# Wider first projections, other PSUM places and two small moves in a sparse-attention block on one core

## The chip, the cores and the metric

The kernel runs on one core of a Trainium2 chip. A core has five engines that work side by side: TensorE (PE in the profile, with its weight loads shown apart as PEld), VectorE (DVE), ScalarE (ACT), GpSimd (POOL) and SyncE (SP), which here issues most of the DMAs. Each engine takes its instructions in order and waits on semaphores for the others. Matmul results land in PSUM, which has eight banks of 512 f32 columns; all other tiles lie in SBUF. The metric is the device time of one execution in microseconds (us).

## What is computed

One layer of a streaming-encoder block on 4096 tokens with 1024 features, in float32:

```python
h = rms_norm(x, norm_g)                 # (4096, 1024)
proj = h @ w_in                         # columns: q 512, k 128, v 128, qi 256, ki 32, wi 8,
                                        #          z_a 512, u_b 512, z_b 512, gates 2 x 1024
q, k = rope(rms_norm(q)), rope(rms_norm(k));  qi, ki = rope(qi), rope(ki)
iscore = sum_h relu(qi_h @ ki.T) * wi_h       # indexer score of every allowed key
idx = top_k(iscore, 256)                      # 256 keys for each query
a = softmax(q @ k[idx].T / 8) @ v[idx] * silu(z_a)
b = pool(u_b) * silu(z_b)                     # trailing means over 2, 4, 8, 16 tokens, a linear map
y = sigmoid(g_a) * (a @ w_branch_a) + sigmoid(g_b) * (b @ w_branch_b)
out = x + y @ w_out
```

A key is allowed if its chunk of 64 tokens does not come after the query's.

## The kernel before

The 4096 tokens are 32 tiles of 128. To come near f32 accuracy, an operand of a product is split into a high part (rounded to a shorter format, by ACT) and a low part (the rest, by DVE or POOL), and a product is three matmuls: high x high, low x high, high x low.

Four phases follow one another. **Phase 1** (`phase1`) normalises the token tiles, transposes them on PE, and projects them on the q, k/v and indexer columns (512, 256 and 296 columns of `w_in`). **The search** (`phase_index`) computes the indexer scores, searches a threshold for each query by iterating, and on the side computes the dense projections (`dense`: gates, pooling). A count of the queries where the threshold is not exact is kept in `cnt`; where it is above zero, `phase_exact` computes those blocks again by 32 rounds of "best eight, then strike them out" (`exact_block`, lines 1266 to 1268). **The attention** (`phase_attention`) and **the output** (`phase_out`) follow.

Within a phase the order on each engine is written by a planner (`Plan`): a step has an engine, an estimated cost, a key (its due time) and the steps that it waits for. `Plan.run` plays the steps through by these estimates and, whenever an engine is free, writes the ready step with the smallest key. So the costs and keys decide the order of the instructions; on the chip the engines then run that order at their real pace. Buffers are rings; a ring's tile gets its address when it is first made, so the order in which tiles are made decides which bank of PSUM they lie in. At the end of phase 1 the planner's remaining work of each engine (`self.left`, `self.late`) is handed to the plan of the search. A tile that lies where a tile of the phase before lay waits for that tile's last reader.

The steps that the change touches:

- `begin` (lines 284 to 313) sets a few constants, keeps PE warm with 18 matmuls on a zeroed tile, and spreads the norm gain `gn` over 128 partitions: ACT's queue loads it as one row into a tile of the ring `x`, PE multiplies it with a row of ones into a PSUM tile `ma`, DVE copies it out.
- Tiles 0 and 1 are projected while the weights arrive. `first` (line 639) is the order in which token tiles and pieces of the weights are loaded on SP's queue; a piece is at most 128 columns wide. `weights` (line 494) loads a piece, has ACT make its high part and DVE its low part; for the first and third q piece POOL makes the low part (`ON_POOL`).
- `piece` (line 515) multiplies a tile with one such piece: 24 matmuls, for each of the three products eight blocks of 128 features. The loop in lines 653 to 661 calls it for tiles 0 and 1 in turn and puts the transposes of tiles 2 and 3 in between. Tiles 2 to 31 go through `project`, whose matmuls are as wide as the column group (512, 256 or 296).
- PSUM in phase 1: two `ma` (two banks each, q and k/v), two `mb` (one bank, indexer), two `pt` (one bank, transposes). `evac` reads `ma` and `mb` and frees them; its last read of `ma` is line 557.
- PSUM in the search: two `ps` of two banks (scores), three `pd` of one (dense), one `pt` (transposes), made in the order that line 814 lists.
- `tables` (line 315) makes the rotation's sines and cosines on DVE and ACT; `evac` needs them before it can free its row buffer (`row`, two of them).
- At the attention's begin DVE sets the tile `ones` (line 1298), and ACT applies an exponential to one column of it (line 1309), so that its table is loaded.

Of the kernel before, what the change touches and what calls it, by code (L numbers as in the profile page):

```python
# [110 lines left out]
ON_POOL = {("q", 0), ("q", 2)}  # L111
# [144 lines left out]
class K:  # L256
# [6 lines left out]
    def consts(self):  # L263
# [6 lines left out]
        self.ii = c1.tile([P, P], I32, name="ii")  # L270
        self.ident = ci.tile([P, P], F32, name="ident")
# [12 lines left out]
    def begin(self, pl, sp, xp, gn):  # L284
# [3 lines left out]
        new = pl.new  # L288
        one = sp.tile([P, 1], F32, name="one")
        row = xp.tile([1, P], F32, name="onerow")  # L290
        s = pl.add("dve", 0.2, -100, lambda: (v.memset(one, 1.0), v.memset(row, 1.0)))
# [13 lines left out]
        x, ma = new("x"), new("ma")  # L305
        g = pl.add("dma", 0.1, -101, lambda: act.dma_start(x.t[0:1], a["norm_g"]), use=[x])

        def spread():
            for f in range(2):
                fs = slice(f * 512, f * 512 + 512)  # L310
                pe.matmul(ma.t[:, fs], row, x.t[0:1, fs], start=True, stop=True)
        g = pl.add("pe", 1.8, -60, spread, [g, s], use=[x, ma])
        return pl.add("dve", 1.2, -60, lambda: v.tensor_copy(gn, ma.t), [g], use=[ma])
# [91 lines left out]
    def phase1(self):  # L405
# [7 lines left out]
        with ExitStack() as es:  # L413
# [80 lines left out]
            def weights(key, j, at):  # L494
# [9 lines left out]
                on = "pool" if (key, j) in ON_POOL else "dve"  # L504
                eng = {"dve": v, "pool": po}[on]
                l = pl.add(on, (2.4 if on == "pool" else 1.15) * n + 0.1, at, lambda: eng.tensor_tensor(
# [8 lines left out]
            def piece(t, key, j, at, prev):  # L515
                m, c = out_of(t, key)
                o, e, hi, lo = pieces[key][j]
# [3 lines left out]
                for i, (x, w, after) in enumerate(((hh, wh, high + [hi]), (hl, wh, low), (hh, wl, [lo]))):  # L521
# [3 lines left out]
                    prev = pl.add("pe", 8 * 0.5e-3 * max(e - o, 64), at, mm, after + [prev], use=[m, hh, hl])  # L525
# [111 lines left out]
            for f in range(2):  # L637
                transp(0, f, -35 + f)
            first = (("q", 0), ("q", 1), ("x", 1), ("q", 2), ("q", 3), ("x", 2), ("kv", 0), ("kv", 1), ("x", 3), ("i", 0), ("i", 1),
                     ("i", 2))  # L640
# [12 lines left out]
            for n, (key, j) in enumerate(x for x in first if x[0] != "x"):  # L653
                for t in range(2):
                    last[t] = piece(t, key, j, n + t * 2.5, last[t])
                    if (key, j) == ("kv", 1):
                        ends[t] = last[t]
                if key == "kv":
                    transp(2, j, n + 2.0)
                elif key == "i" and j < 2:  # L660
                    transp(3, j, n + 4.0)
# [1559 lines left out]
```

## Time and profile before

| | us |
|---|---|
| median of 3 runs | 4133.96 (4132.86 to 4137.76) |
| profiled execution | 4135.42 |
| its span, first to last instruction | 4133.7 |
| PE busy | 4012.3 (97%) |
| DVE busy | 3251.7 (79%) |
| ACT busy | 2259.5 (55%) |
| POOL busy | 2022.9 (49%) |

An instruction's row gives its start and its length in us, the engine, the line of the kernel, the operation, its tiles as output <- inputs, their shapes, and how many were merged into the row; in brackets stands how long the engine idled before it and what it was released by. A `q` behind an engine's name marks its sequencer or DMA queue. Matmuls overlap, so the time of one in a stream is read from the distance between starts. The granted clock is the share of full speed at which PE was allowed to run.

### The profile page before, as it was taken

How to read it: one execution, taken by the hardware profiler on the slowest of the kernel's cores; microseconds unless marked ns; L12 is line 12 of the kernel's file. 1: busy time of each engine (PE TensorE's matmuls, PEld its weight loads, DVE VectorE, ACT ScalarE, POOL GpSimd, SP SyncE). 2: the span in 40 equal slices, each digit the busy share in tenths (PEclk: the TensorE clock that was granted, in tenths of full speed). 3: DMA queues.
4: the chain of work that ended last, by engine and by line, in shares of the span. 5: the costliest groups of instructions: out<-in, count | busy, mean ns of one | idle time of the engine just before them, and what ended most of it. 6: DMA issues, size and time to landing. Idle time of an engine off the chain costs nothing.

```text
span 4133.7 us, 64472 instructions
## 1 busy us (share of the span) xinstructions
PE 4012.3 (97%) x23202; PEld 3074.1 (74%) x23203; DVE 3251.7 (79%) x6399; ACT 2259.5 (55%) x3163; POOL 2022.9 (49%) x1618
## 2 busy tenths in 40 slices
PE   9999999999999999999989999999999999999999
PEld 9999888787777777788756666666666666887787
DVE  5555688888888888778779999999999996556654
ACT  4444578786777877877645555555554543111221
POOL 3555312212213223010018889999999994334653
PEclk9999999999999999999979999999999999999999
DMA  6876644544545345666554433333222215887543
GB/s 183 301 244 237 201 168 173 171 167 168 177 164 194 135 172 180 199 234 237 199 142 87 76 76 61 64 62 54 56 54 43 40 25 167 284 254 239 190 158 122
DMA packets 515846, 636.87 MB, mean 154 GB/s; under 512 B 230593, under 2 KB 365377, under 8 KB 511554
## 3 DMA queue, kind: packets, MB, share of 16 engines
q1 hardware_dynamic: 490432, 609.51, 47.1%
q10 hardware_dynamic: 25090, 23.21, 2.5%
q8 instruction: 183, 3.00, 0.3%
q14 instruction: 141, 1.16, 0.1%
HBM read 408.96 MB, written 191.76 MB: 145 GB/s over the span
## 4 chain that ended last, share of the span: by engine, by line
PE 37%; DVE 6%; issue 4%; DMA 1%; POOL 1%; SPq 1%; ACT 0%; ACTq 0%; DVEq 0%; POOLq 0%
PE pv L1686 9%; PE st L1634 8%; PE p L2139 7%; PE p L1990 7%; PE ps L1566 4%; DVE jk L1575 4%; DVE tt L1647 1%; PE pt L1734 1%; PE pt L395 1%; DMA qm<-maxD 1%; PE st L395 0%; PE st L1854 0%; POOL g L2020 0%; DVE w L1897 0%; DMA g<-w_out 0%
## 5 line engine op out<-in xcount | busy, mean ns | idle before, releaser
L1665 POOL TENSOR_TENSOR acc<-acc,tt 128x1024 f32<-128x1024 f32 x388 | 927.7, 2391 | 64.0 <-ACT tt L1646 36.9
L1646 ACT ACTIVATE tt<-tt 128x1024 f32<-128x1024 f32 (+1 forms) x544 | 561.1, 1034 | 549.7 <-DVE tt L1647 518.9
L1197 PE MATMUL pd<-h,wgh 128*128 128x512 f32 x1792 | 708.8, 396 | 9.9 <-DMA h<-hD 9.9
L1196 PE MATMUL pd<-h,wgh 128*128 128x512 f32 x1792 | 714.1, 399 | 3.9 <-issue 3.8
L908 DVE SCALAR_TENSOR_TENSOR ring<-rl,wi,ring 128x1024 f32<-128x1024 f32 (+7 forms) x624 | 702.1, 1170 | 15.7 <-ACT rl L906 12.4
L1198 PE MATMUL pd<-h,wgl 128*128 128x512 f32 x1792 | 707.0, 395 | 0.0
L906 ACT ACTIVATE rl<-ps 128x1024 f32<-128x1024 f32 (+7 forms) x624 | 535.5, 887 | 190.0 <-PE ps L903 69.4
L1647 DVE TENSOR_TENSOR tt<-st,bT 128x1024 f32<-128x1024 f32 (+1 forms) x504 | 600.8, 1193 | 13.1 <-PE st L1634 13.1
L993 ACT ACTIVATE sg<-ring,tk 128x2048 fp8e4<-128x2048 f32 (+9 forms) x322 | 485.1, 1508 | 63.0 <-DVE tk L981 34.4
L1686 PE MATMUL pv<-tt,vv 128*64 128x256 f32 x4224 | 516.2, 386 | 1.4 <-ACT ov L1707 1.4
L1575 DVE CUSTOM_DVE_ANT_1 jk<-ps,bias,mf 128x1024 bf16<-128x1024 f32 (+3 forms) x408 | 469.6, 1151 | 17.1 <-PE ps L1566 15.3
L1686 PEld LDWEIGHTS pv<-tt,vv 128*64 128x64 f32 x4224 | 286.5, 137 | 168.7 <-issue 35.4
L1197 PEld LDWEIGHTS pd<-h,wgh 128*128 128x128 f32 x1792 | 339.8, 190 | 84.1 <-DMA h<-hD 16.6
L1196 PEld LDWEIGHTS pd<-h,wgh 128*128 128x128 f32 x1792 | 340.0, 190 | 78.6 <-issue 4.2
L1198 PEld LDWEIGHTS pd<-h,wgl 128*128 128x128 f32 x1792 | 339.4, 189 | 75.9
L903 PE MATMUL ps<-kis,qT 128*128 128x512 f32 (+3 forms) x1136 | 345.3, 390 | 37.9 <-ACT rl L906 37.7
L1990 PE MATMUL p<-g,w 128*128 128x512 f32 x1488 | 345.5, 394 | 1.7 <-DVE g L1913 1.7
L1990 PEld LDWEIGHTS p<-g,w 128*128 128x128 f32 x1488 | 279.4, 188 | 67.6 <-DVE g L1913 2.1
L2139 PE MATMUL p<-w,g 128*128 128x512 f32 x1344 | 314.3, 396 | 4.0 <-ACT g L2143 3.1
L2139 PEld LDWEIGHTS p<-w,g 128*128 128x128 f32 x1344 | 253.5, 189 | 64.6 <-ACT g L2143 3.5
L1566 PE MATMUL ps<-kh,qh 64*128 64x512 f32 (+3 forms) x1320 | 265.5, 419 | 29.3 <-DVE mf L1575 26.5
L1110 POOL COPY halo<-u 128x16 f32<-128x16 f32 x32 | 11.2, 350 | 575.5 <-ACT u L1104 575.5
(364 smaller groups left out, 7012.3 us busy)
## 6 DMA issues: line engine op xcount, KB each, us to landing
h<-hD SPq DMA_DIRECT2D x384, 512.0 KB
g<-gD SPq DMA_DIRECT2D x80, 512.0 KB
hlD<-rhl SPq DMA_DIRECT2D x31, 1216.0 KB
gD<-sgm SPq DMA_DIRECT2D x128, 256.0 KB
q<-hlD SPq DMA_DIRECT2D x61, 512.0 KB
x<-x SPq DMA_DIRECT2D x32, 512.0 KB
hD<-hh SPq DMA_DIRECT2D x32, 512.0 KB
hD<-hl SPq DMA_DIRECT2D x32, 512.0 KB
```

The source lines that it names most:

```text
L906: r = pl.add("act", 0.05 + n * 0.834e-3, k_, lambda ps=ps, rl=rl, n=n: act.activation(rl.t[:, :n], ps.t[:, :n], AF.Relu), [m], use=[ps, rl])
L908: prev[o] = pl.add("dve", 0.1 + n * 1.04e-3, k_, lambda rl=rl, o=o, n=n, h=h: v.scalar_tensor_tensor(acc[:, o:o + n], rl.t[:, :n], self.wi ...
L1196: pe.matmul(out, wh.t[:, k], r1, start=(k == 0), stop=False)
L1197: pe.matmul(out, wh.t[:, k], r2, start=False, stop=False)
L1198: pe.matmul(out, wl.t[:, k], r1, start=False, stop=(k == KT - 1))
L1575: v.tensor_tensor_reduce(out=jk.t[:, :2 * (hi - lo) * P].rearrange("p (t n) -> p t n", t=2), in0=flat().rearrange("p (t n) -> p t n", t=2) ...
L1646: act.activation(tt.t[:, 0:n], tt.t[:, 0:n], AF.Exp)
L1647: ad = last_ve[0] = pl.add("dve", 0.07 + 0.54 * n, key, lambda: v.tensor_tensor(tt.t[:, 0:n], s.t[:, 0:n], bc(bt.t[:, 2 * p:2 * p + n, Non ...
L1665: gp.tensor_tensor(acc.t, first, tt.t, op=OP.add)
L1686: pe.matmul(pv.t[64 * f:64 * f + 64], vv[:, k, 64 * g:64 * g + 64], T[u, p].t[:, k % 2, 2 * f:2 * f + 2], start=(k == 0), stop=(k == b))
L1990: pe.matmul(p.t, blk[i].t[:, k, ms], two(x[k // 2][j].t, F32R)[:, k % 2], start=(k == i == j == 0), stop=(k == 3 and i == 1))
L2139: pe.matmul(p.t, quarter(Q.t, x, F32R)[:, k], blk[y].t[:, k], start=(fresh and k == x == y == 0), stop=(k == 3 and x == 1), skip_group_che ...
```

## The change

- `begin` no longer spreads the gain on PE. SP's queue loads it straight to all partitions, with a DMA that reads the same row 128 times, second in the queue.
- `ON_POOL` is gone: DVE makes all low parts of the weights.
- `piece` takes several weight pieces at a time: tiles 0 and 1 multiply q in two halves of 256 columns, k/v in one of 256, the indexer's columns in one of 296. The weights still arrive in pieces of 128 columns, the token tiles 1, 2 and 3 at other places between them; the planner's cost of a block is 0.4575 ns per column instead of 0.5 ns. The transposes of tiles 2 and 3 come behind the k/v and the indexer blocks.
- The list that makes the search's PSUM tiles begins with `pt` and has `ps0` fifth instead of first.
- `ones` lies in the constants of the whole kernel and is set in the search.
- The 32 rounds of the exact search are a loop instead of 64 instructions written out.

```diff
@@ begin
+        self.ones = cp.tile([P, 64], F32, name="ones")
...
-        x, ma = new("x"), new("ma")
-        g = pl.add("dma", 0.1, -101, lambda: act.dma_start(x.t[0:1], a["norm_g"]), use=[x])
-
-        def spread():
-            for f in range(2):
-                fs = slice(f * 512, f * 512 + 512)
-                pe.matmul(ma.t[:, fs], row, x.t[0:1, fs], start=True, stop=True)
-        g = pl.add("pe", 1.8, -60, spread, [g, s], use=[x, ma])
-        return pl.add("dve", 1.2, -60, lambda: v.tensor_copy(gn, ma.t), [g], use=[ma])
+        return pl.add("dma", 1.7, -95, lambda: dma(gn, bass.AP(tensor=a["norm_g"].tensor, offset=a["norm_g"].offset,
+                                                              ap=[[0, P], [1, D]])))
@@ weights
-                on = "pool" if (key, j) in ON_POOL else "dve"
-                eng = {"dve": v, "pool": po}[on]
-                l = pl.add(on, (2.4 if on == "pool" else 1.15) * n + 0.1, at, lambda: eng.tensor_tensor(
+                l = pl.add("dve", 1.15 * n + 0.1, at, lambda: v.tensor_tensor(
                     lo[:, :, o:e], raw, hi[:, :, o:e].bitcast(F32), op=OP.subtract), [h])
@@ piece
-            def piece(t, key, j, at, prev):
+            def piece(t, key, js, at, prev):
                 m, c = out_of(t, key)
-                o, e, hi, lo = pieces[key][j]
+                parts = [pieces[key][j] for j in js]
+                o, e = parts[0][0], parts[-1][1]
+                hi, lo = [x[2] for x in parts], [x[3] for x in parts]
...
-                for i, (x, w, after) in enumerate(((hh, wh, high + [hi]), (hl, wh, low), (hh, wl, [lo]))):
+                for i, (x, w, after) in enumerate(((hh, wh, high + hi), (hl, wh, low), (hh, wl, lo))):
...
-                    prev = pl.add("pe", 8 * 0.5e-3 * max(e - o, 64), at, mm, after + [prev], use=[m, hh, hl])
+                    prev = pl.add("pe", 8 * 0.4575e-3 * (e - o), at, mm, after + [prev], use=[m, hh, hl])
@@ phase1
-            first = (("q", 0), ("q", 1), ("x", 1), ("q", 2), ("q", 3), ("x", 2), ("kv", 0), ("kv", 1), ("x", 3), ("i", 0), ("i", 1),
-                     ("i", 2))
+            first = (("q", 0), ("q", 1), ("q", 2), ("x", 1), ("q", 3), ("kv", 0), ("kv", 1), ("x", 2), ("i", 0), ("i", 1),
+                     ("i", 2), ("x", 3))
...
-            for n, (key, j) in enumerate(x for x in first if x[0] != "x"):
+            for n, (key, js) in enumerate((("q", (0, 1)), ("q", (2, 3)), ("kv", (0, 1)), ("i", (0, 1, 2)))):
                 for t in range(2):
-                    last[t] = piece(t, key, j, n + t * 2.5, last[t])
-                    if (key, j) == ("kv", 1):
+                    last[t] = piece(t, key, js, 2 * n + t * 2.5, last[t])
+                    if key == "kv":
                         ends[t] = last[t]
-                if key == "kv":
-                    transp(2, j, n + 2.0)
-                elif key == "i" and j < 2:
-                    transp(3, j, n + 4.0)
+                        transp(2, t, 2 * n + t + 2.0)
+                    elif key == "i":
+                        transp(3, t, 2 * n + t + 4.0)
@@ phase_index
-        for name, i in (("ps", 0), ("pd", 0), ("pd", 1), ("pd", 2), ("pt", 0), ("ps", 1)):
+        for name, i in (("pt", 0), ("pd", 0), ("pd", 1), ("pd", 2), ("ps", 0), ("ps", 1)):
             pl.have(name, i)
...
+        v.memset(self.ones, 1.0)
@@ exact_block
-            for _ in range(32):
+            with tc.For_i(0, 32):
                 v.max(m8, work)
                 v.match_replace(out=work, in_to_replace=m8, in_values=work, imm_value=-3.3e38)
@@ phase_attention
-        ones = sp.tile([P, 64], F32, name="ones")
-        v.memset(ones, 1.0)
+        ones = self.ones
```

More of the change, by code (lines that the diff above doesn't have):

```diff
@@ L110 @@
 WARM = 9
-ON_POOL = {("q", 0), ("q", 2)}
 HLD = 40.0
@@ L289, in begin @@
         one = sp.tile([P, 1], F32, name="one")
-        row = xp.tile([1, P], F32, name="onerow")
-        s = pl.add("dve", 0.2, -100, lambda: (v.memset(one, 1.0), v.memset(row, 1.0)))
+        s = pl.add("dve", 0.1, -100, lambda: v.memset(one, 1.0))
         pl.add("act", 1.6, -100, lambda: act.activation(one, one, AF.Sqrt), [s])
```

## The prediction

> **What bounds the kernel now.** I read the page's head first, then busy time by stretch, then the instructions in order of time where a stretch stands out.
>
> ```profile
> span 4133.7 us, 64472 instructions
> ```
> ```profile
> 14.00:53.58 39.58, 39.52 (x354) 39.34 (x353) 24.84 (x44) 15.77 (x29) 6.62 (x17) 1.00 0.63 184
> 53.58:73.91 20.33, 20.33 (x107) 20.33 (x106) 3.94 (x7) 3.34 (x7) 1.79 (x3) 0.54 0.06 19
> 73.91:452.60 378.69, 378.69 (x2416) 345.77 (x2414) 212.54 (x424) 179.24 (x443) 210.36 (x536) 1.00 0.75 257
> 452.60:461.50 8.90, 5.12 (x14) 3.91 (x13) 6.01 (x13) 3.83 (x15) 6.57 (x20) 0.62 0.29 113
> 461.50:2074.60 1613.10, 1563.03 (x6843) 1250.72 (x6841) 1315.48 (x3516) 1218.69 (x1617) 312.17 (x281) 0.99 0.53 183
> ```
>
> The columns are the stretch, its length, busy time (with instructions) of PE, PEld, DVE, ACT and POOL, granted clock, DMA share and GB/s. The first two stretches are the first two token tiles, multiplied while their weights still arrive; the third is tiles 2 to 31, the fourth the hand-over to the search, the fifth the search with the dense projections. PE has no gap from 14 to 452.6 us, so in this part PE alone sets the time and whatever shortens its work moves everything behind it. Yet in the second stretch PE runs at a granted clock of 0.54. What it does there:
>
> ```profile
> 17.09 1.06 PE L524 MATMUL ma<-wqh,hh 128*128 128x128 f32 x8
> 17.98 1.06 PE L524 MATMUL ma<-wqh,hl 128*128 128x128 f32 x8
> ...
> 53.58 1.01 PE L524 MATMUL mb<-wih,hh 128*128 128x40 f32 x8
> 54.44 1.05 PE L524 MATMUL mb<-wih,hl 128*128 128x40 f32 x8
> ...
> 73.91 0.78 PE L401 MATMUL ma<-wqh,hh 128*128 128x512 f32 x1
> ...
> 80.43 0.60 PE L473 MATMUL pt<-ident,x 128*128 128x128 f32 x4
> ...
> 84.09 0.38 PE L401 MATMUL mb<-wih,hh 128*128 128x296 f32 x1
> ...
> 87.45 0.39 PE L401 MATMUL ma<-wqh,hh 128*128 128x512 f32 x1
> ...
> 93.05 0.60 PE L473 MATMUL pt<-ident,x 128*128 128x128 f32 x4
> 93.41 0.37 PE L401 MATMUL ma<-wkvh,hh 128*128 128x256 f32 x1
> ...
> 96.23 0.60 PE L473 MATMUL pt<-ident,x 128*128 128x128 f32 x4
> ```
>
> Eight matmuls of 128 columns take 0.89 us (17.09 to 17.98), 0.111 us each; eight of 40 columns take 0.86 us (53.58 to 54.44), though they move a third of the data. So with one weight load per matmul, 128 columns or fewer cost the load, not the columns. In the steady tiles 24 matmuls of 256 columns take 2.82 us (93.41 to 96.23), 24 of 296 take 3.36 us (84.09 to 87.45): 0.118 and 0.140 us each. Twice the columns for the same price, and the clock falls right behind the first 40-column block, with PE never idle.
>
> **The change part by part.**
>
> *Wider first projections.* Tiles 0 and 1 now do their 24 matmuls on q in two halves of 256 columns instead of four quarters, k/v in one of 256 instead of two, the index columns in one of 296 instead of 128 + 128 + 40. Removed per tile: 4 + 2 + 3 = 9 pieces of 24, for both tiles 432 matmuls, 18 x 24 x 0.1115 = 48.2 us at full clock. Added: 2 x (2 + 1) x 2.82 + 2 x 3.36 = 23.6 us. On top comes the half-clock stretch: in 20.33 us at 0.54 PE did work worth 11.0 us, so 9.3 us are clock; and tile 2's q still starts cold, 6.52 us (73.91 to 80.43) against 5.60 us (87.45 to 93.05), 0.9 us more. The new blocks move 256 columns or more, as the steady tiles do at clock 1.00, so I take both as gone. By PE work alone the gain is 24.6 + 9.3 + 0.9 = 34.8 us.
>
> *Whether the weights keep up.* PE gets faster, so DMA, ACT and DVE may become late.
>
> ```profile
> 4.56 1.06 ACT L451 ACTIVATE sq<-x 128x1024 bf16<-128x1024 f32 x1 [1.51 <-DMA x<-x]
> ...
> 7.16 1.23 DVE L313 COPY gn<-ma 128x1024 f32<-128x1024 f32 x1 [5.34 <-PE ma L311]
> ...
> 8.59 1.99 ACT L503 ACTIVATE wqh<-h 128x1024 fp32r<-128x1024 f32 x2
> ...
> 9.68 3.62 DVE L460 SCALAR_TENSOR_TENSOR x<-x,rs,gn 128x512 f32<-128x512 f32 x2
> 9.71 2.39 POOL L506 TENSOR_TENSOR wql<-h,wqh 128x1024 fp32r<-128x1024 f32 x1 [8.15 <-ACT wqh L503]
> ...
> 13.23 1.21 DVE L506 TENSOR_TENSOR wql<-h,wqh 128x1024 fp32r<-128x1024 f32 x1
> ...
> 14.04 0.52 PEld L524 LDWEIGHTS ma<-wqh,hh 128*128 128x128 f32 x4 [0.20 <-ACT hh L475]
> ...
> 25.05 0.69 DVE L476 TENSOR_TENSOR hl<-pt,hh 128x512 fp32r<-128x512 f32 x1 [0.84 <-ACT hh L475]
> ```
> ```profile
> 0.00:5.00 5.00, 3.66 (x6) 2.00 (x8) 0.51 (x6) 2.14 (x5) 0.98 (x7) 1.00 0.67 195
> 5.00:10.00 5.00, 5.00 (x10) 2.70 (x9) 2.40 (x8) 2.23 (x5) 0.29 (x1) 1.00 1.09 318
> 10.00:15.00 5.00, 4.50 (x22) 3.11 (x22) 5.00 (x5) 2.06 (x4) 2.10 (x1) 1.00 1.15 321
> ```
> ```profile
> h<-w_in SPq DMA_DIRECT2D x8, 512.0 KB
> ...
> h<-w_in SPq DMA_DIRECT2D x1, 160.0 KB
> ```
>
> The DMA engines are full almost from the start: 0.98 and 1.59 MB in the first two stretches, so 2.57 MB by 10 us, and 0.321 MB per us behind that. SP's queue now issues x0, the gain broadcast (512 KB written instead of 4 KB), q0, q1, q2, x1, q3, kv0, kv1, x2, three index pieces, x3. The second q quarter then ends at 2.10 MB, 8.5 us; the fourth, with x1 ahead, at 3.67 MB, 13.4 us; the last index piece at 6.46 MB, 22 us. In exchange PE's broadcast and DVE's copy of 1.23 us (7.16) are gone, which held the mean behind it (the square had ended by 5.6 us), and the two low parts that POOL made move to DVE. That costs DVE 2 x 1.21 us (13.23), but POOL's 2.39 us also stood across DVE: two scalings took 3.62 us (9.68) while POOL worked from 9.71. I book the move at nothing on the path: DVE is busy 24.8 of 39.6 us in the first stretch; without that cover it costs its 2.4 us.
>
> First matmul: 8.5 + 1.0 for the high part (8.59: two in 1.99 us) = 9.5 us, instead of 14.04. Behind it stand 23.6 us and six groups of transposes of tiles 1 to 3 at 0.36 us (93.05 to 93.41), 25.8 us. The second q half waits for its weights: the first ends at 12.3, the fourth quarter's high part at 14.4, 2.1 us. The rest comes early enough (the index block starts after 30 us, its weights land at 22). So tile 2 would start at 9.5 + 25.8 + 2.1 = 37.4 us. From both sides: 35.3 us without a wait; 46 us if tile 1's transposed low part is as late as now (25.05 + 0.69, where PE would want it near 17.3, 8.4 us). I take 40, nearer the work than the old order, whose lateness came in part from POOL standing across DVE. The gain: 73.91 - 40 + 0.9 = 34.8 us, the same as by PE work alone, since the earlier first matmul (4.5) and the waits (4.6) cancel; bounds 28.8 and 39.5.
>
> *Other PSUM places.*
>
> ```profile
> 455.55 0.82 DVE L557 TENSOR_TENSOR row<-ma,ss 128x640 f32<-128x640 f32 x1 [1.18 <-POOL ss L390]
> ...
> 456.48 0.76 PE L1196 MATMUL pd<-h,wgh 128*128 128x512 f32 x1 [3.78 <-issue]
> ```
>
> At the hand-over PE idles 3.78 us. It starts right behind DVE's last read of tile 31's accumulator (455.55 + 0.82 = 456.37): rings get their banks in the order of the list in line 814, and with `ps0` first, `pd0`, the dense stage's first output, lies on the upper bank of that accumulator. With `pt` first, `pd0` lies on the second bank, where phase 1 (its banks too go in order of first use, and without the broadcast both transpose buffers come first) has a transpose buffer, long free; tile 31's accumulator then lies under `ps0`, wanted only at the first scores. So the 3.78 us go, and the cold start with them: 461.50 - 456.48 at about half rate, 2.5 us. Bounds 0 (the search's own chain sets the next wait) and 6.3; I take 5, since PE is busy 1563.0 of 1613.1 us in the stage.
>
> *Ones early, search as a loop.*
>
> ```profile
> 2076.03 1.28 ACT L1309 ACT_TABLE_LOAD   x1 [0.82 <-DMA q<-hlD]
> ...
> 2079.12 0.11 DVE L1298 MEMSET ones<- 128x64 f32 x1 [3.19 <-DVEq L1215]
> ...
> 2079.26 0.20 ACT L1309 ACTIVATE ones<-ones 128x1 f32<-128x1 f32 x1 [1.95 <-DVE ones L1298]
> ...
> 2080.05 0.43 DVE L1398 CAST kh<-st 64x256 fp32r<-64x256 f32 x1 [0.82 <-ACT kl L1398]
> ```
> ```profile
> L1215 ACTq EVENT_SEMAPHORE  x2: 17/17/17, 2075.6 to 2075.7; - x2
> L1215 DVEq EVENT_SEMAPHORE  x2: 21/21/21, 2078.8 to 2078.9; - x2
> ...
> L1215 ACTq COMPARE_BRANCH  x1: 50/50/50, 2075.2 to 2075.2; - x1
> L1215 DVEq COMPARE_BRANCH  x1: 72/72/72, 2075.9 to 2075.9; - x1
> ```
>
> The skipped exact search costs DVE 2.9 us between its branch (2075.9) and the next instruction behind it (2078.8), ACT 0.4 us. ACT, whose table is loaded at 2077.31, waits 1.95 us for DVE's memset, and behind it stand the copies that free PE's bank. The memset moves to the search (0.11 us there, where DVE is busy 1315 of 1613 us). The copies start 1.95 us earlier; DVE's first cast, at 2080.05 behind ACT's second copy, moves by 1.05 if DVE's branch stays as long, by 1.8 if 62 instructions less bring it near ACT's 0.4. From both sides: 0.5 lost to loop code, 3.2 won if DVE's wait were all on the path. I take 1.5.
>
> Sum: 34.8 + 5 + 1.5 = 41.3 us off the profiled execution's 4135.4 (span 4133.7 and 1.7 around it; the median of the runs is 4134.0, 1.4 less): **4094 us**. Likeliest case's own range: gains of 28.8 + 0 - 0.5 and 39.5 + 6.3 + 3.2, 4086 to 4107.
>
> [...] The clock of 0.54 came while PE was busy 20.33 of 20.33 us. [...] The trace has both: a gap (3.78 us, then 0.62) and a dip without one.
>
> **The rivals.** (a) *The tables become late.* Rotation needs tables that DVE makes; until then tiles 0 and 1 hold both row buffers, and PE stops two tiles on for want of a free accumulator. Now DVE idles most of 53.58 to 73.91 (3.94 us busy), time that disappears; against it, DVE's instructions there wait for PE, not for data. If PE waits some 10 us: 4104. (b) *The dip stays*, set off by something else, or by PE waiting for weights at the start: 9.3 + 0.9 us, 4104. For it: a gap of 3.78 us was enough at 456; against: the waits I find are 2.1 us. (c) *The projections turn out bound by the arrival of weights*, so the change doesn't do what it says: half of 34.8 is lost, 4111. Against: 6.46 MB land by 22 us. (d) *Slower:* the search's order is written anew from what phase 1 leaves on each engine; a worse interleaving of its 18 groups lengthens PE's waits. They are 50.1 us of 1613.1 now; from 91 us the gain is gone, and 2.6 us more per group (47 us) give 4141. Against: what is left over comes from tiles 30 and 31, which the change doesn't touch.
>
> **How the numbers follow.** Likeliest 0.70, (a) 0.12, (b) 0.10, (c) 0.04, (d) 0.04. The range of 8 in 10 takes the likeliest's bounds, (a) and (b) and most of (c), widened at the low side for both late gains together: 4080 to 4113. A run of this kernel tells 0.2%, 8 us, from no change. Faster 0.95, within 0.2% 0.02, slower 0.03.
>
> **What would show it.** Right: tile 2's 512-column q starts at 36 to 46 us at clock 1.00, no stretch of 0.5 before it; the first dense matmul follows the last transpose of phase 1 without a gap and the fourth stretch is at 1.00; ACT's exp starts by 2077.5 less the gain before it. Wrong: PE waits at tiles 3 to 5 with `ma` or `mb` as the tile, a half-clock stretch before tile 2, or PE's waits in the search well above 50 us.

## The result, and the profile after

The kernel after takes 4088.9 us (median of 4 runs, 4081.3 to 4094.4), the kernel before on the same chip 4133.4 us. The ratio is 0.9891, 95% interval 0.9872 to 0.9911: 44.5 us less. The forecast was 4094. The profiled execution took 4089.8 us, 45.6 less than the one of before. One execution of the first kernel under "The experiments" took 9565.5 us at a granted clock of 1.00; why is not known, and it is left out of that kernel's figures.

Stretches of the kernel after: length, busy time of PE, PEld, DVE, ACT and POOL (with instructions), granted clock, DMA share, GB/s. They are the first two tiles, tiles 2 to 31, and the search with the dense projections; under them, from the timeline, PE's steps at the borders.

```profile
span 4088.1 us, 63978 instructions
```
```profile
12.06:39.53 27.47, 27.47 (x217) 27.47 (x217) 22.40 (x40) 17.37 (x33) 5.25 (x18) 0.94 0.99 294
39.53:418.35 378.82, 378.16 (x2417) 344.30 (x2415) 220.26 (x434) 176.58 (x446) 211.34 (x537) 1.00 0.75 258
...
418.35:2032.50 1614.15, 1559.56 (x6856) 1246.31 (x6854) 1323.33 (x3528) 1223.29 (x1629) 321.18 (x300) 0.99 0.53 183
```
```profile
12.06 1.18 PE L516 MATMUL ma<-wqh,hh 128*128 128x256 f32 x8 [1.63 <-ACT wqh L495]
...
14.74 1.91 PE L516 MATMUL ma<-wql,hh 128*128 128x256 f32 x8
...
39.53 0.48 PE L393 MATMUL ma<-wqh,hh 128*128 128x512 f32 x1
...
418.29 0.22 PE L387 MATMUL mb<-identr,rhk 128*128 128x128 f32 x1
418.35 0.44 PE L1188 MATMUL pd<-h,wgh 128*128 128x512 f32 x1
```

Tile 2's q starts at 39.53 us instead of 73.91, and the first dense matmul, at 418.35 instead of 456.48, follows phase 1's last transpose without a gap. From the same rows of both profiles, and from the first starts of the later stages, the 45.6 us are made up like this:

| stage | before, us | after, us | gain |
|---|---|---|---|
| start of tile 2's q | 73.91 | 39.53 | 34.4 |
| tile 2's q to phase 1's last step | 378.6 | 378.8 | -0.2 |
| last step to first dense matmul | 4.01 | 0.06 | 3.9 |
| first to last dense matmul | 1617.7 | 1613.7 | 4.0 |
| to the attention's first softmax logits | 36.7 | 36.5 | 0.2 |
| attention, to the output's first matmul | 1353.6 | 1350.6 | 3.0 |
| output | 669.2 | 668.9 | 0.3 |

The attention's 3.0 us are no part of the change: with the same attention code its stage took 1350.6 to 1364.1 us in the profiled executions of the kernels below, and the profile after happens to hold the shortest. Most of that scatter goes with the granted clock. Counted in steps of 3.41 us at half clock within this stage, the kernel after has 6.8 (1350.6 us), the kernel before 7.8 (1353.6), the wide projections alone 13.4 (1362.6) and the narrow blocks made 128 wide 14.9 (1364.1); from the first to the last of these, 8.1 steps go with 13.5 us.

The search took 1609.1 to 1617.7 us in these profiles. At its begin the half-rate stretch of before (456.48 to 461.5), worth 2.5 us there, is gone: the 400th dense matmul comes 121.5 us behind the first instead of 123.8. By the 1600th nothing of it can be told, 481.5 us in both, and the stage's totals don't separate the kernels that begin it at half clock (1609.1 to 1617.7 us) from the others (1609.2 to 1615.3). So of the stage's 4.0 us, 2.5 are seen where they arise, and whether they last to its end is not shown.

Two things in the profile after were not in the forecast. First, ACT at the kernel's begin:

```profile
2.28 1.28 ACT L1300 ACT_TABLE_LOAD   x1
3.58 0.20 ACT L1300 ACTIVATE ones<-ones 128x1 f32<-128x1 f32 x1
...
5.74 1.28 ACT L375 ACT_TABLE_LOAD   x1
...
9.74 1.32 ACT L467 ACTIVATE hh<-pt 128x512 fp32r<-128x512 f32 x2 [0.69 <-PE pt L465]
10.96 2.00 ACT L495 ACTIVATE wqh<-h 128x1024 fp32r<-128x1024 f32 x2
```

The exponential that reads `ones` (line 1300, the attention's) is executed at 3.58 us: its tile is now set at the kernel's begin, nothing else holds it, and in the compiled program it stands right behind. ACT loads the exp table at 2.28 (1.28 us) and the table for the square root again at 5.74 (1.28 us), in front of tile 0's norm. Second, the attention's begin, with the branch over the exact search (DVE, line 1207):

```profile
2036.85 0.20 POOL L1291 MEMSET neg<- 128x128 f32 x1 [127.23 <-DVEq L1207]
...
2037.28 0.38 ACT L1389 ACTIVATE kl<-st 64x256 fp32r<-64x256 f32 x1 [1.90 <-POOL neg L1291]
```
```profile
L1207 DVEq EVENT_SEMAPHORE  x2: 21/21/21, 2036.7 to 2036.8; - x2
...
L1207 DVEq COMPARE_BRANCH  x1: 72/72/72, 2033.8 to 2033.8; - x1
```
```profile
2070.05 1.28 ACT L1637 ACT_TABLE_LOAD   x1 [2.12 <-DVE tt L1638]
```

DVE branches at 2033.8 and reaches the next instruction at 2036.7, 2.9 us, as before. The first of ACT's two copies (`kh`) does start earlier, 2.50 us behind the last dense matmul's end instead of 4.80. The second (`kl`) comes 4.77 us behind it instead of 5.07 and waits 1.90 us: POOL's first memset waits for DVE to come out of the branch, and the copy for POOL. The exp table, no longer loaded here ahead of time, is loaded at 2070.05 in front of the first softmax.

### The profile page after: what moved, and what is told of

It reads as the page before. It is cut to its first block, busy times and chain, and to the rows that moved or that the text cites. A ratio compares the mean times of both kernels' runs of the same rounds, so it can differ in the third digit from the quotient of the medians.

```text
span 4088.1 us, 63978 instructions
## 1 busy us (share of the span) xinstructions
PE 3964.7 (97%) x22958; PEld 3028.6 (74%) x22959; DVE 3255.0 (80%) x6399; ACT 2259.6 (55%) x3165; POOL 2021.8 (49%) x1616
## 5 line engine op out<-in xcount | busy, mean ns | idle before, releaser
L1566 DVE CUSTOM_DVE_ANT_1 jk<-ps,bias,mf 128x1024 bf16<-128x1024 f32 (+3 forms) x408 | 469.5, 1151 | 16.1 <-PE ps L1557 14.3
L1677 PEld LDWEIGHTS pv<-tt,vv 128*64 128x64 f32 x4224 | 285.6, 137 | 169.1 <-issue 34.8
L894 PEld LDWEIGHTS ps<-kis,qT 128*128 128x128 f32 x1136 | 206.8, 189 | 116.8 <-ACT rl L897 76.3
```

The source lines that it names most:

```text
L894: pe.matmul(ps.t[:, s:e], t.t[:, h], self.kis[:, o + s:o + e], start=True, stop=True)
L1566: v.tensor_tensor_reduce(out=jk.t[:, :2 * (hi - lo) * P].rearrange("p (t n) -> p t n", t=2), in0=flat().rearrange("p (t n) -> p t n", t=2) ...
L1677: pe.matmul(pv.t[64 * f:64 * f + 64], vv[:, k, 64 * g:64 * g + 64], T[u, p].t[:, k % 2, 2 * f:2 * f + 2], start=(k == 0), stop=(k == b))
```

## The experiments

Two kernels were timed in several rounds, the first and the last. The others ran once, in this order as shown: 256 and 40 columns 4091.8 us, narrow blocks side by side 4116.3 and (128 wide) 4113.1, wide projections alone 4110.0, list alone 4129.2, old list 4093.2, broadcast back 4103.5, POOL 4097.1, ones 4098.0, no exact search 4090.6. A single total scatters by several us, so these are read by their stages.

### The 40-column block made 128 wide

```
 def piece(t, key, j, at, prev):          # kernel before
     o, e, hi, lo = pieces[key][j]
+    o = min(o, e - 128)
```

> The kernel before, with one thing changed: in tiles 0 and 1 the last index block computes columns 168 to 296 (128 wide; 88 columns are computed a second time, to the same values) instead of columns 256 to 296 (40 wide). Same number of matmuls and weight loads. My theory (the 40-column matmuls themselves set off the half clock, and cost no less than 128 columns): the stretch from the first of these blocks to tile 2's q shows clock 1.00 and takes 20.33 x 0.54 = 11.0 us instead of 20.33, tile 2's 512-column q starts at about 64.6 us instead of 73.91 and runs at its warm rate (5.6 us to the next transposes instead of 6.52); in all 9 to 10.5 us less, about 4124. Rival 1 (something else sets the dip off, PE being busy throughout): the stretch stays at about 0.54, tile 2's q at 73.9 within 0.5 us, time unchanged. Rival 2 (any matmul of 128 columns or fewer does it, after long enough): the dip comes a few us later and lasts as long, tile 2's q at 70 to 74.

```profile
53.58 1.06 PE L525 MATMUL mb<-wih,hh 128*128 128x128 f32 x8
54.47 1.06 PE L525 MATMUL mb<-wih,hl 128*128 128x128 f32 x8
...
65.09 0.48 PE L401 MATMUL ma<-wqh,hh 128*128 128x512 f32 x1
```

No half-clock stretch before tile 2: eight matmuls of 128 columns take 0.89 us throughout, and tile 2's q starts at 65.09, 8.8 us earlier. The median is 4123.6 against 4132.8, ratio 0.9976 (0.9966 to 0.9986). Three times the columns made the kernel faster by 9.2 us; the 40-column blocks had been the cause of the dip.

### A block of 256 and one of 40 in the kernel after

```
-for n, (key, js) in enumerate((..., ("i", (0, 1, 2)))):
+for n, (key, js) in enumerate((..., ("i", (0, 1)), ("i", (2,)))):
```

> The kernel after, with the index columns of tiles 0 and 1 in a block of 256 and one of 40 instead of one of 296. My theory: the 40-column blocks cost 24 x 0.11 us each and bring the clock down although PE never idles. PE work alone adds 2 x 24 x (0.118 + 0.108 - 0.140) = 4.1 us; a half-clock stretch begins about 2 us into the first 40-column block and lasts one or more times 3.4 us, 1.7 us lost in each, so that tile 2's q starts at 45.3 to 49 us instead of 39.53, and the total is 6 to 9 us longer. Rival (narrow blocks do not touch the clock): clock 1.00 from 25 us on, tile 2's q at 43.6 us.

```profile
34.77 1.05 PE L516 MATMUL mb<-wih,hh 128*128 128x40 f32 x8
35.66 1.05 PE L516 MATMUL mb<-wih,hl 128*128 128x40 f32 x8
...
40.72 1.05 PE L516 MATMUL mb<-wih,hh 128*128 128x40 f32 x8
...
43.81 0.48 PE L393 MATMUL ma<-wqh,hh 128*128 128x512 f32 x1
```

My theory fell, the rival's 43.6 us holds: the 40-column blocks cost what they cost (0.89 us for eight), and the clock stays up behind them. So narrow blocks alone are not enough. What differs from before is what surrounds them: 256-column matmuls here, 128-column ones there.

The moments at which the clock changes say more. Stretches cut at them, granted clock third from the end, in the kernel before and in the kernel after:

```profile
51.95:55.36 3.41, 3.41 (x34) 3.41 (x32) 3.26 (x8) 0.87 (x2) 0.00 (x0) 1.00 0.83 287
55.36:75.84 20.48, 20.48 (x95) 20.09 (x95) 3.19 (x7) 3.07 (x6) 1.89 (x3) 0.50 0.05 5
...
454.72:461.54 6.82, 5.06 (x13) 3.93 (x14) 4.56 (x8) 2.68 (x10) 6.41 (x19) 0.50 0.22 81
```
```profile
9.63:13.04 3.41, 1.68 (x13) 1.40 (x13) 3.36 (x5) 3.17 (x5) 0.00 (x0) 1.00 1.13 335
13.04:16.45 3.41, 3.41 (x19) 3.41 (x17) 2.97 (x10) 2.29 (x4) 0.00 (x0) 0.51 1.21 290
```

Half clock lasts 20.48 us, 6.82 and 3.41: six, two and one times 3.413. The two falls of before, at 55.36 and 454.72, are 399.36 us apart, 117.0 times 3.413. So in these two profiles the clock changes on a grid of 3.413 us: all 31 changes of before and all 21 of after lie on it to within 0.01 us. A fall came with and without idle PE: PE was busy 3.41 of 3.41 us in the step ahead of the one at 55.36, and 1.68 ahead of the one at 13.04.

The columns that passed in the step ahead of a fall, from the rows (128-column matmuls pass 8 x 128 / 0.89 = 1150 per us, 40-column ones 8 x 40 / 0.86 = 372, 256-column ones 8 x 256 / 0.94 = 2180): before, 51.95 to 55.36, 1.63 us of the first and 1.78 of the second kind, 744 per us. In the kernel with only the new list, below, 51.39 to 54.80, 2.20 and 1.21 us, 874 per us, and the clock fell at 54.80. In the kernel just shown the poorest step, 39.16 to 42.57, holds 1.21 us of 256 columns, a group of transposes (512 columns) and 1.85 us of 40 columns, 1125 per us, and the clock stayed. This was the new theory for the next two.

### Narrow blocks side by side, 40 and 128 wide

```
-    last[t] = piece(t, key, js, 2 * n + t * 2.5, last[t])       # kernel with 256 + 40
+    last[t] = piece(t, key, js, 12 if js == (2,) else 2 * n + t * 2.5, last[t])
+    if js == (2,):
+        last[t] = piece(t, key, js, 12, last[t])
```

and for the second kernel `o = min(o, e - 128)` in `piece` as above.

> The kernel after, with the index columns of tiles 0 and 1 in a block of 256 and one of 40, the 40-column blocks put behind everything else of the two tiles and each computed twice, so that PE does 5.3 us of 40-column matmuls, 0.7 us of transposes and 5.3 us of 40-column matmuls in a row, never idle. A new theory, made from the runs so far: the clock changes at multiples of 3.413 us only (55.36 to 75.84 us before are 6.0 of them, the same grid at the hand-over), and is taken down where the columns that went through PE in the last such stretch are few: 740 to 870 per us in the stretches that led to a fall, 1080 and more in those that did not; 40-column matmuls pass 370 per us, 128-column ones 1150, 256-column ones 2170. By it this kernel must fall to half clock 3.4 to 7 us after the first 40-column matmul and stay there until 512-column matmuls have filled a stretch: PE work at full clock puts tile 2's q at about 49 us, the half clock at 53 to 58 us. Rival (what counts is the change from one block form to another, or chance): clock 1.00 throughout, tile 2's q at 48 to 50 us. Rival 2 (only an idle PE brings the clock down): the same as rival 1.

> As the kernel with the 40-column blocks side by side and computed twice, but with these blocks 128 columns wide (columns 168 to 296; what is computed again has the same values): the same number of matmuls and weight loads at the same place. Theory of the grid of 3.413 us and the columns per us: 128-column matmuls pass 1150 per us, more than any stretch that led to a fall, so the clock stays at 1.00, eight matmuls take 0.89 us, and tile 2's q starts at 48 to 50 us instead of 56.25. Rival (it is the long run of small blocks, or the block that is computed twice, that brings the clock down): half clock in it, tile 2's q at 53 us or later.

The kernel with 40 columns, then the one with 128, each from the timeline of PE; the stretches are of the first.

```profile
37.39 0.96 PE L516 MATMUL mb<-wih,hh 128*128 128x40 f32 x8
...
40.98 1.88 PE L516 MATMUL mb<-wih,hl 128*128 128x40 f32 x8
...
56.25 0.77 PE L393 MATMUL ma<-wqh,hh 128*128 128x512 f32 x1
```
```profile
37.35:40.76 3.41, 3.41 (x33) 3.41 (x32) 3.20 (x11) 1.15 (x2) 0.00 (x0) 1.00 0.54 197
40.76:61.24 20.48, 20.48 (x87) 19.42 (x87) 11.56 (x18) 3.07 (x6) 4.75 (x8) 0.50 0.34 104
```
```profile
48.81 0.45 PE L393 MATMUL ma<-wqh,hh 128*128 128x512 f32 x1
```

As the theory had it: PE is busy without a break, yet the clock falls at 40.76, 3.4 us into the 40-column blocks, and comes back 20.48 us later, once 512-column matmuls have run; tile 2's q starts at 56.25. With the same number of matmuls at 128 columns the clock is 1.00 from 2 to 80 us and tile 2's q starts at 48.81. Between these two kernels width decides, not idleness and not the length of the run of small blocks.

The whole profiles of before and after say more. I count the columns of the matmuls that start in each whole step of the grid (a few records may be missing), over the steps whose matmuls all use 128 rows. In the 18 steps ahead of a fall at most 900 columns per us start; of the 1559 others at full clock four have 900, and the rest 938 or more. PE's busy time doesn't order the steps so: in the kernel with only the new list PE was busy 3.41 of 3.41 us from 51.39 to 54.80, passed 868 to 874 columns per us, and the clock fell; in the kernel after it was busy only 1.6 of 3.41 us from 985.91 to 989.32, six matmuls of 512 columns started, 900 per us, and the clock stayed at 1.00. So in these two profiles the clock fell at 900 per us and less, and stayed at 900 and more. It is no general figure: in the attention, whose score matmuls use 64 rows, steps with up to 1650 columns per us led to a fall. Whether the columns are what is counted, or something that goes with them, these runs don't settle.

The kernels with 40 and with 128 columns also show how little a total tells: the second is 7.4 us ahead at tile 2's q and only 3.2 us in the total (4113.1 against 4116.3), since its attention had 14.9 half-clock steps against 10.6 and took 1364.1 us against 1360.0.

### The wide projections alone

```
 the edits of `piece` and of its loop, on the kernel before; nothing else
```

> The kernel before, with only the wider first projections (256, 256 and 296 columns); the order of the loads, the broadcast on PE, POOL's two low parts, the list of PSUM places, the ones and the unrolled search stay as before. My theory (the gain at the start is width: fewer matmuls, and no narrow block to bring the clock down): no half-clock stretch before tile 2, which starts its q at 14.04 + 25.8 us of PE work plus 0 to 6 us of waits for weights, 40 to 46 us (30 or so of the 34.4 us won there); the hand-over to the search keeps its gap of 3.8 us and its cold stretch; time about 4101 to 4107. Rival (the other order of loads, the broadcast by DMA and the low parts on DVE carry a good part): PE waits for weights 8 us or more in the first tiles, tile 2's q at 48 us or later.

```profile
17.79 1.20 PE L526 MATMUL ma<-wqh,hh 128*128 128x256 f32 x8 [0.42 <-ACT wqh L503]
20.64 0.63 PE L473 MATMUL pt<-ident,x 128*128 128x128 f32 x4 [1.65 <-issue]
...
43.54 0.48 PE L401 MATMUL ma<-wqh,hh 128*128 128x512 f32 x1
...
426.41 0.76 PE L1197 MATMUL pd<-h,wgh 128*128 128x512 f32 x1 [3.06 <-issue]
```
```profile
16.78 2.39 POOL L506 TENSOR_TENSOR wql<-h,wqh 128x1024 fp32r<-128x1024 f32 x1 [4.68 <-ACT wqh L503]
```
```profile
17.02 2.16 DVE L387 TENSOR_TENSOR rt<-ry 128x1 f32<-128x1 f32 x1
```

Tile 2's q at 43.54: width gives 30.4 of the 34.4 us won at the start, the other order of loads, the broadcast by DMA and the low parts on DVE the other 4.0. The first matmul stays at 14.04. PE waits 0.42 us for the second half of q's weights. The 1.65 us at 20.64 are another wait, for tile 1's scaling: a DVE instruction ahead of it in tile 1's norm takes 2.16 us (17.02), where its neighbours take 0.16, and ends as POOL's low part does (16.78 + 2.39 = 19.17). The kernel before has the same pair of rows. The gap at the hand-over stays, 3.06 us. The one run took 4110.0 us, 3 more than expected; its attention stage was 1362.6 us, 9 longer than that of before with the same code, with 13.4 half-clock steps against 7.8.

### The PSUM list alone, the old list in the kernel after, and the broadcast back on PE

```
-for name, i in (("ps", 0), ("pd", 0), ("pd", 1), ("pd", 2), ("pt", 0), ("ps", 1)):
+for name, i in (("pt", 0), ("pd", 0), ("pd", 1), ("pd", 2), ("ps", 0), ("ps", 1)):
```

on the kernel before; the reverse on the kernel after; and, as the third, `begin` of before (row of ones, PE, DVE's copy) in the kernel after, with the new list.

> The kernel before, with only the list that gives the search its PSUM places in the new order (pt, pd, pd, pd, ps, ps). My theory (the first dense matmul waits for whatever phase 1 left in its bank): in this kernel the broadcast on PE takes the first accumulator, so phase 1's banks are, in order of first use, pt, ma, ma, pt, ma, ma, mb, mb, and tile 31 sits in the first of the two accumulators, banks 1 and 2. With the new list the dense stage's first output lies on bank 1, still tile 31's: the gap of about 3.8 us in front of the first dense matmul stays, 3.3 to 4.2 us, with the half-rate stretch behind it, and the time is unchanged. Rival (putting the transposition place first is enough by itself): the first dense matmul follows phase 1's last step without a gap, 4 to 6 us less in that place.

> The kernel after, with the PSUM places of the search in the old order (ps, pd, pd, pd, pt, ps). My theory (an operation waits for what phase 1 left in its own bank): phase 1's banks are now, in order of first use, pt, pt, ma, ma, ma, ma, mb, mb, tile 31 in banks 4 and 5; with the old order the dense stage's first output lies on bank 2 (tile 30's, long read) and the search's transposition buffer on bank 5, the upper bank of tile 31's accumulator, which DVE reads until some 3.5 us after phase 1's last step. So the first dense matmul follows without a gap, and the fourth instruction of the search, the turn of a key into that buffer, waits instead: 2 to 3 us of idle PE there, perhaps with one half-clock stretch of 3.4 us behind it; everything later 2 to 5 us later than in the kernel after. Rival 1 (the gap is removed by the broadcast having left PE, the list is idle): no gap anywhere, same times as after. Rival 2 (the old list brings the old gap back as it was): 3 to 4 us in front of the first dense matmul.

> The kernel after, with the gain broadcast on PE and copied by DVE again, as before (so the accumulators of phase 1 change places, and the load of 512 KB is gone). My theory: the first matmul on q starts 0.5 to 2 us later than 12.06 us, since the mean behind it waits for DVE's copy of 1.23 us; tile 2's q at 40 to 42 us; at the hand-over tile 31 sits in banks 1 and 2 again, where the new list has put the dense stage's first output, so PE idles 3 to 4 us in front of the first dense matmul, and a half-clock stretch of 3.4 or 6.8 us follows. Together the first dense matmul is 4 to 7 us later than 418.35. Rival (the new list alone removes the gap, wherever tile 31 sits): no gap, first dense matmul later only by what the start loses.

In this order, PE's timeline at the hand-over; of the first also the row at which its 40-column blocks begin, and, from the stretches, its half clock behind them:

```profile
53.59 1.01 PE L524 MATMUL mb<-wih,hh 128*128 128x40 f32 x8
...
457.62 0.76 PE L1196 MATMUL pd<-h,wgh 128*128 128x512 f32 x1 [3.34 <-issue]
```
```profile
54.80:78.69 23.89, 23.89 (x105) 23.02 (x105) 5.99 (x12) 3.28 (x7) 1.90 (x3) 0.50 0.12 34
```
```profile
418.24 0.44 PE L1188 MATMUL pd<-h,wgh 128*128 128x512 f32 x1
...
421.62 0.25 PE L387 MATMUL pt<-identr,k 128*128 128x128 f32 x1 [2.48 <-DVE row L549]
```
```profile
45.16 0.48 PE L401 MATMUL ma<-wqh,hh 128*128 128x512 f32 x1
...
426.26 0.48 PE L1196 MATMUL pd<-h,wgh 128*128 128x512 f32 x1 [3.19 <-issue]
```

The new list alone leaves the gap (3.34 us). The old list in the kernel after moves it to the first transposition, 2.48 us, released by DVE's last read of tile 31's accumulator (`row`, line 549). With the broadcast back on PE the accumulators shift by one and the gap is there again in spite of the new list (3.19 us). So what counts is which bank tile 31 sits in: list and broadcast remove the gap together, neither by itself. The third kernel's start was slower than I expected, 45.16 instead of 40 to 42: DVE makes three low parts between the two scalings of tile 0 there, the first matmul comes at 16.45, and one grid step of half clock follows.

### The low parts on POOL again

```
-l = pl.add("dve", 1.15 * n + 0.1, at, lambda: v.tensor_tensor(
+on = "pool" if (key, j) in {("q", 0), ("q", 2)} else "dve"
+l = pl.add(on, (2.4 if on == "pool" else 1.15) * n + 0.1, at, lambda: eng.tensor_tensor(
```

> The kernel after, with the low parts of the first and third quarter of q's weights on POOL, as before. My theory (POOL's 2.4 us take no less of the path than DVE's 1.2, because both stand across each other): tile 2's q within 1.5 us of 39.53, DVE's scalings of x that fall into POOL's time take 1.5 to 2.6 times as long as now. Rival (the move to DVE cost DVE 2.4 us that PE then waited for): tile 2's q 2 us or more earlier.

```profile
9.17 2.66 POOL L498 TENSOR_TENSOR wql<-h,wqh 128x1024 fp32r<-128x1024 f32 x1 [7.62 <-ACT wqh L495]
12.99 2.48 POOL L498 TENSOR_TENSOR wql<-h,wqh 128x1024 fp32r<-128x1024 f32 x1 [1.15 <-ACT wqh L495]
```
```profile
8.20 1.41 DVE L452 SCALAR_TENSOR_TENSOR x<-x,rs,gn 128x512 f32<-128x512 f32 x2
10.33 1.42 DVE L468 TENSOR_TENSOR hl<-pt,hh 128x512 fp32r<-128x512 f32 x2 [0.72 <-ACT hh L467]
...
14.76 0.73 DVE L379 TENSOR_TENSOR rt<-ry 128x1 f32<-128x1 f32 x1
```

Tile 2's q starts at 39.54, as in the kernel after, but the two don't compare directly: this kernel has no half clock at its start, the kernel after has one step of it. Against the kernels without that step and with the low parts on DVE (39.03 with the old list, 39.00 without the exact search) 39.54 is 0.5 us later. So the move to DVE gains some 0.5 us, where I had booked nothing.

The stretching that I gave as the reason is there: the small instruction at 14.76 takes 0.73 us, where its neighbours take 0.16, and ends as POOL's second low part does (12.99 + 2.48 = 15.47). Tile 1's scaling then starts at 16.10 instead of 15.70, and PE waits 0.29 us for it at 18.79. Tile 0's scalings are all but over when POOL starts, and DVE's subtractions at 10.33, which read PSUM, are not stretched inside POOL's 2.66 us: 0.69 us each, in the kernel after 0.68. The kernel before bears it out. Of its two scalings that took 3.62 us together (9.68), the first takes 2.96 us and ends at 12.65, behind POOL's low part (9.71 to 12.10), and the second 0.74. So in these rows three of DVE's instructions on SBUF tiles that begin beside POOL's subtraction end with it or behind it: 0.73 us instead of 0.16 (14.76), in the kernel before 2.16 instead of 0.16 (17.02) and 2.96 instead of 0.74 (9.68).

### Ones in the attention again, and no exact search

```
-ones = self.ones
+ones = sp.tile([P, 64], F32, name="ones")
+v.memset(ones, 1.0)
```

and, as a kernel of its own, the kernel after without the call of `phase_exact`.

> The kernel after, with the ones (and so the first exp, which reads them) allocated and set in the attention again, as before. In the kernel after ACT loads the exp table at 2.28 us and the sqrt table again at 5.74 us, 1.28 us that stand in front of the square root for tile 0. My theory: without it the first q matmul starts 0.5 to 1.3 us earlier than 12.06, but PE then waits for the second half of q's weights, so tile 2's q is 0 to 0.8 us earlier than 39.0 to 39.5; in the attention ACT again loads the exp table at its begin and waits for DVE's memset behind DVE's branch, so the first matmul of the index scores' recomputation (line 1557) comes 0 to 1 us later, counted from the last dense matmul, than the 12.0 us of the kernel after; the exp table's load of 1.28 us in front of the first exp of the softmax is gone there. Rival (the hoisted table load is hidden at the start, since weights are late anyway): first q matmul within 0.2 us of 11.8 to 12.1.

> The kernel after without the exact search that is skipped on these inputs: its instructions and the branch over them are left out, so a query whose threshold fails would not be computed again. My theory (in the kernel after the attention's first copies wait for DVE to come out of the branch, 2.9 us): the first matmul of line 1557 starts 8 to 10 us behind the last dense matmul instead of 12.0. Rival (the attention's begin is set by its loads and by PE's turns; the branch is hidden): 11.5 to 12.5 us.

With the ones in the attention the first q matmul comes at 11.13 instead of 12.06: the pulled-up table load costs 0.9 us there. Tile 2's q comes at 40.73 all the same, later than expected, since one grid step of half clock falls on 16.1 to 19.5 us, where PE has work: 1.7 us more than in the last kernel below, which has the same first matmul and no half clock. Attention: the first matmul of line 1557 comes 12.23 us behind the last dense matmul, in the kernel after 11.93, in the kernel before 12.22. So setting the ones early gains 0.3 us, and costs the first softmax 1.0 us (its first exp 38.8 us behind the last dense matmul instead of 37.8).

Without the exact search (its begin of the attention, all engines):

```profile
2029.80 0.20 POOL L1290 MEMSET neg<- 128x128 f32 x1 [122.74 <-PE pd L1189]
...
2032.07 0.38 ACT L1388 ACTIVATE kh<-st 64x256 fp32r<-64x256 f32 x1 [1.69 <-PE st L387]
2032.35 0.36 ACT L1388 ACTIVATE kl<-st 64x256 fp32r<-64x256 f32 x1
```

ACT's two copies follow each other without a wait, and line 1557 starts 10.4 us behind the last dense matmul: between my 8 to 10 and the rival's 11.5 to 12.5. The branch costs 1.5 us there, and 2.1 us at the attention's first weighted sum (46.1 us instead of 48.2); with it gone, the copies and turns behind are the next bound.

### Table load and idle PE at the start

```
-act.activation(ones[:, 0:1], ones[:, 0:1], AF.Exp, scale=0.0)
+    act.activation(qm.t[0:66, 4 * g:4 * g + 4], pt.t[0:66], AF.Copy)     # in turn_maxima
+    if u == 4:
+        act.activation(warmx, warmx, AF.Exp, scale=0.0)
...
+for _ in range(5):                       # behind tile 0's transposes
+    pe.matmul(spare.t[:, 0:512], self.identr, W["q"][0][:, 0:4, 0:128], start=True, stop=True)
```

> The kernel after with two things changed: the exp that loads ACT's table no longer stands where it is pulled to the kernel's begin, but behind the fifth copy of turned maxima in the attention, where ACT is idle 2.1 us; and five matmuls of 512 columns (their result is overwritten) fill PE's idle time in front of the first q matmul. My theory: the first q matmul 0.3 to 1.3 us earlier than 12.06; no half-clock stretch at the start; tile 2's q at 38.2 to 39.2 us instead of 39.53, no more, since PE waits there for the second half of q's weights; the first exp of the softmax 1 to 2 us earlier, counted from the attention's first turn; in all 1.5 to 3.5 us less than the kernel after, about 4086, which is at the edge of what a comparison can tell. Rival (both are hidden): the same times within 0.3 us at both places.

First q matmul at 11.13, no half clock at the start, tile 2's q at 39.04; first exp 37.6 us behind the last dense matmul instead of 38.8, but the first weighted sum at 48.2 as before. The start and the first exp came as expected; the total, expected at about 4086, did not: the median is 4091.0. Of what was won at these places only the 0.5 us at tile 2's q reach a later stage. The start without half clock does not show that the five matmuls did it, since the kernel without the exact search has none either. The ratio to the kernel before is 0.9903 (0.9883 to 0.9923), no better than the 0.9891 of the kernel after.

## Why the prediction was right, point by point

- **Wider first projections, 34.8 us forecast, 34.2 measured** (34.4 until tile 2's q, -0.2 behind it: the cold start of 0.9 is gone, PE now waits 0.7 us once for DVE's last read of an `ma`, and the 0.4 us that are left lie within this stage's scatter, 377.7 to 380.2 us in the other kernels). The price per matmul and the count were right: from 12.06 to 39.53 PE worked 27.47 us, of which 1.7 us are the loss of the step at half clock; 25.8 us are left, the forecast's sum. The step that failed is the first matmul at 9.5 us, "8.5 + 1.0 for the high part": it reckoned with the weights' arrival alone. Before the second high part ACT copies tile 0's transposes (9.74), which wait for tile 0's norm, and that for the table loaded a second time (5.74). That 40 us came out so near 39.53 is luck: I had added 2.6 us to the worked-out 37.4 for tile 1's low part being late, and for that PE did not wait, it has no idle time from 12.06 to 39.53; the late first matmul happened to cost as much.
- **The wait of 2.1 us for the second half of q's weights** was 1.06 us in the kernel with the old list, whose start is the same but for the clock; in the profile after it is hidden behind PE at half clock. So this dip costs 0.5 us, not 1.7: tile 2's q is at 39.53 with it, at 39.03 and 39.00 without, in the kernels with the old list and without the exact search.
- **The half-clock stretch, 9.3 + 0.9 us.** It is gone, and padding alone won 9.2 us of the kernel before. The reason I gave, that the clock falls behind the 40-column block, was incomplete: it took the 128-column work around it as well, which left 744 columns per us in the step ahead of the fall. The rival that the dip stays came true on a small scale, behind PE's idle time at the start, for one grid step.
- **PSUM places, 5 us taken, 0 to 6.3 as bounds.** The mechanism was right: the gap's 3.9 us are gone, and no later stage became longer for it. The cold start's 2.5 us are gone at the search's begin, but the search's later rows don't show them, so the deduction from 6.3 to 5 is neither confirmed nor refuted. That list and broadcast act only together was in the argument, and three kernels bear it out.
- **Ones and loop, 1.5 us forecast, 0.2 to 0.3 measured.** The step that failed is "the copies start 1.95 us earlier": the first did, by 2.3 us, the second by 0.3. The wait for `ones` had stood in front of another that ends at nearly the same time: for DVE out of its branch, through POOL's memset. The loop did not shorten the branch: 2.9 us before and after.
- **POOL's low parts at nothing:** the reason, POOL standing across DVE, is borne out (2.96 us instead of 0.74 in the kernel before, 0.73 instead of 0.16 with the low parts on POOL again); the move gains some 0.5 us.
- **Rivals (a), (c), (d):** in tiles 2 to 31 PE is busy 378.16 of 378.82 us, so no late table cost more than the 0.7 us named; the start kept up with its weights except for the one wait named above; the search did not get longer.

Terms that the change explains come to 34.4 - 0.2 + 3.9 + 2.5 + 0.2 = 40.8 us, against 41.3 forecast; without the 2.5 us, which are shown at the search's begin only, they are 38.3. The other 4.8 to 7.3 us of the profiled execution lie in the scatter of search, attention and output.

## What to carry to other kernels

With one weight load for each matmul, 40 columns cost here what 128 do (0.107 against 0.111 us), and 256 hardly more (0.118). Behind many narrow ones the clock stood at 0.50 for 20.48 us here, under the work after them too, although PE was busy without a break. So ask of a stretch not only whether PE is busy, but how many columns pass. A bank's free time is set by who used it last, so an order of allocation that looks indifferent decides which instruction stands at a hand-over (here for 2.48 to 3.78 us). A constant that is set earlier sets free what waits only for it, and a planner or compiler may then pull that forward into a place where it costs more (here 0.3 us won at the attention's begin, 0.9 us lost at the first q matmul and 1.0 at the first softmax).

## What the runs showed of the hardware

- In the profiles of before and after the clock granted to PE changed on a grid of 3.413 us (two falls of before 117.0 steps apart). It fell while PE was busy 3.41 of 3.41 us, at 744 columns per us in the kernel before and 874 in the one with only the new list; it stayed at 1125 in the kernel with 256 and 40 columns and at 1150 in the one with the 40-column block made 128 wide. With matmuls of 128 rows, at most 900 per us start in every step ahead of a fall in before and after.
- The longest stretch at half clock in before and after is one that the change doesn't touch: at the attention's begin, 40.96 us (twelve steps; 2079.47 to 2120.43 before, 2037.22 to 2078.18 after), with PE busy 29.5 us of them.
- Once down, it stayed down under work that had not brought it down. In the kernel before, two rows of PE's timeline:

```profile
58.76 1.91 PE L524 MATMUL mb<-wih,hl 128*128 128x128 f32 x8
60.47 1.91 PE L524 MATMUL mb<-wil,hh 128*128 128x128 f32 x8
```

Eight matmuls of 128 columns take 1.71 us here, 600 columns per us, and the clock stays at half, though the same matmuls had run at 1.00 from 14 us on.

- Branching over the skipped exact search costs DVE 2.9 us in the kernels before and after (idle time of DVE up to its next instruction 3.19 us in before, 3.47 with only the new list, 3.65 with only the wide projections), whether its 32 rounds stand in the program as 64 instructions or as a loop of two.
